# High and low V of one head as one stationary operand in attention's value products

## The chip, the cores and the metric

The kernel runs on one core of a Trainium2 chip. The core has five engines that run side by side, each through its own queue in order: TensorE (PE in the profile; PEld is its weight load), VectorE (DVE), ScalarE (ACT), GpSimd (POOL) and SyncE (SP), which here issues nearly all DMA transfers. They wait for one another through semaphores. The metric is the device time of one execution in microseconds; it is given as the median of several runs, and the profile is of one further execution.

## What is computed

Two layers on 512 tokens of width 1024, in float32. The change lies in the token mixer of the first layer, a stick-breaking attention with 16 heads of 64 columns; no softmax is taken. Cut to what matters:

```python
def stick_breaking_attention(q, k, v):
    ...
        z = jnp.einsum('bhtd,bhsd->bhts', q[:, :, q0:kend], k[:, :, :kend]).astype(jnp.float32) * scale
        ...
        before = s_idx < t_idx
        log_beta = jax.nn.log_sigmoid(z)
        log_1m = jnp.where(before, jax.nn.log_sigmoid(-z), 0.0)
        later = lax.cumsum(log_1m, axis=3, reverse=True) - log_1m
        a = jnp.where(before, jnp.exp(log_beta + later), 0.0)
        outs.append(jnp.einsum('bhts,bhsd->bhtd', a.astype(v.dtype), v[:, :, :kend]))
```

The last line, the product of the weights `a` with `v`, is what the change is about. Around it stand a QKV projection, an output projection, a SwiGLU feed-forward, a gated MLP mixer as the second layer's token mixer, a second feed-forward, and adaLN modulation before and after each.

## The kernel before

All large products run in TensorE's fp32r format on operands that are split in two: `split` (line 89) writes a rounded high part with ScalarE (line 93) and the remainder as a low part with VectorE (line 94). `mm3` (line 81) multiplies two such operands in three passes: high by high, high by low, low by high. Each pass is one matmul with its own weight load.

The kernel first normalizes and transposes the tokens, projects V's first half and q and k of head pair 0, then enters attention, in which heads are worked in eight pairs: one pair fills 128 columns of V (two heads of 64). V comes out of the projection in two halves of 512 columns; `v_evac` (line 568) splits each into tiles `Vh` and `Vl` of [128 tokens, two token blocks, 512 columns].

For a pair, `attend(i)` (line 721) gives four steps:

- `scores` (line 738): matmuls `z`, a sigmoid on ScalarE into `ga` (line 759), scans on VectorE into `left` (line 764), their differences on VectorE back into `ga` (line 769): the weights `a`.
- `flip` (line 775): transposes the weights of one head into the bank `tw`, and splits them into `ar` (high on ScalarE, low on VectorE).
- `values` (line 789): for each block of key tokens `jj`, `mm3` with 128 columns of V as the stationary operand and `ar` as the moving one, 128 or 256 columns of tokens wide, summed in the bank `av[h]`. The stationary columns are those of both heads; for each head `h` only the 64 rows of its own are used.
- `finish` (line 804): ScalarE copies for each head the 64 rows of its own from `av[h]` to `f` (line 810, `of` in the profile), and `split` writes the pair's output tile `o`.

Attention's queue on TensorE is written out by hand: with `pe["chain"]` set, every matmul is ordered behind the one before. The loop over pairs (from line 841) runs, for pair i: `flip(LATE)`, fillers, scores of pair i + 1 (first part), fillers, `values(LATE)`, `flip(EARLY[0])`, scores (second part), `values(EARLY[0])`, `flip(EARLY[1])`, scores (third part), `values(EARLY[1])`, `finish`. Each of the three `values` stages is called for both heads in turn; the text calls such a stage of two heads one call. `LATE` and `EARLY[0]` have, for a head, one block of 128 and one of 256 columns, `EARLY[1]` two of 256.

The fillers (line 674) are the projections of q and k of the later pairs (bank `pqk`) and, when these are done, a first part of the output projection (bank `y`). A filler step may also start a step of the adaLN modulation (`bg`, line 268): loads `rawada`, and a multiply-add into `G`, `A` and `B` on VectorE. Weights are loaded as `raw` and split into `wh` and `wl`, three tiles ahead.

On VectorE and ScalarE the order is set by a scheduler at build time, which takes the instruction that by its own estimates is ready first; so a new instruction also moves its neighbours.

Of the kernel before, what the change touches and what calls it, by code (L numbers as in the profile page):

```python
# [9 lines left out]
F32R = mybir.dt.float32r  # L10
AF = mybir.ActivationFunctionType
ALU = mybir.AluOpType

P = 128
T = 512
NT = T // P
# [9 lines left out]
def trunk(ctx: ExitStack, tc: tile.TileContext, A: dict, out: bass.AP):  # L26
# [16 lines left out]
    def nm(s):  # L43
        uid[0] += 1
        return f"{s}_{uid[0]}"

    def slot(dt, name, a=2, b=512):
        return s4.tile([P, a, b], dt, tag="s4", name=nm(name))

    def bank(name, tag="b"):  # L50
        return psum.tile([P, 512], F32, tag=tag, bufs=6 if tag == "b" else 2, name=nm(name))

    dve, act = nc.vector, nc.scalar
    pe = {"prev": None, "chain": False}

    def pe_op(b):

        if pe["chain"] and pe["prev"] is not None:
            order(b, pe["prev"])
        pe["prev"] = b  # L60

    def order(b, before):
        tc.add_manual_dep(
            b.ins, before.ins.name,
            mybir.DependencyInfo(mybir.DependencyClass.NoSync, mybir.DependencyReason.DATA),
            reason="order",
        )

    def mm(o, l, r, start, stop, after=None):
        b = nc.tensor.matmul(o, l, r, start=start, stop=stop, skip_group_check=True)  # L70
        pe_op(b)
        if after is not None:
            order(b, after)
# [3 lines left out]
    def transpose(o, i):  # L77
        last_tp[0] = nc.tensor.transpose(o, i, ident)  # L78
        pe_op(last_tp[0])

    def mm3(o, lh, ll, rh, rl, start, stop):
        mm(o, lh, rh, start, False)
        mm(o, lh, rl, False, False)
        mm(o, ll, rh, False, stop)
# [4 lines left out]
    def split(hi, lo, src, hi_dve=False):  # L89
        if hi_dve:  # L90
            dve.tensor_copy(hi, src)
        else:
            act.activation(hi, src, AF.Copy)  # L93
        dve.tensor_tensor(lo, src, hi.bitcast(F32), ALU.subtract)  # L94
# [453 lines left out]

    hT = new_hT()

    Vh = [[slot(F32R, "Vh") for _ in range(2)] for _ in range(2)]
    Vl = [[slot(F32R, "Vl") for _ in range(2)] for _ in range(2)]

    def v_step(vb, hf, k, w):
        for part in range(2):
# [11 lines left out]

    def v_evac(vb, hf):
        for tt in range(NT):
            split(Vh[hf][tt // 2][:, tt % 2, :], Vl[hf][tt // 2][:, tt % 2, :], vb[tt][:])  # L570

    onec = oneb[:, 0:1]

# [45 lines left out]
    vb = [bank("v0") for _ in range(NT)]  # L619
# [31 lines left out]
    st0.__exit__(None, None, None)  # L651
    fwork["raw"] = ctx.enter_context(tc.tile_pool(name="wraw2", bufs=2))
    v_evac(vb, 0)
    o8 = []
    with tc.tile_pool(name="att", bufs=1) as att, tc.tile_pool(name="att2", bufs=2) as att2:
# [65 lines left out]
        def attend(i):  # L721

            weights = {}
            vc = slice(i % 4 * P, (i % 4 + 1) * P)
            vhf = i // 4

            def layout(js):
                offs, N = {}, 0
                for j in js:
                    offs[j] = N
                    N += T - P * j
                return offs, N

            def scores(js):

                q, kt = qk[i]  # L740
                offs, N = layout(js)
                for j in js:
                    o, n = offs[j], T - P * j
                    js_ = slice(j * P, (j + 1) * P)
                    for t, (a, b) in enumerate(((0, 0), (0, 1), (1, 0))):
                        for h in range(2):
                            r = slice(64 * h, 64 * h + 64)
                            mm(
                                zb[h][:, o : o + n], q[r, a, js_], kt[r, b, j * P : T],
                                j == js[0] and t == 0, t == 2,  # L750
                            )
                wide = js[0] != 2
                g = att.tile(
                    [P, 2, T + 4 if wide else 260], F32, tag=f"ga{wide}",
                    bufs=3 if wide else 1, name=nm("ga"),
                )
                with tc.issue_after(table.ins):
                    for h in range(2):
                        last_act[0] = act.activation(g[:, h, :N], zb[h][:, :N], AF.Sigmoid, scale=-1.0)

                for h in range(2):
                    for e, j in enumerate(js):
                        o, n = offs[j], T - P * j
                        dve.tensor_tensor_scan(  # L764
                            left[:, h, o + 1 : o + e + 1 + n], g[:, h, o - e : o + n],
                            tri[:, 1 - e : n + 1], 1.0, ALU.mult, ALU.max,
                        )
                M = N + len(js) - 1
                dve.tensor_tensor(g[:, :, :M], left[:, :, :M], left[:, :, 1 : M + 1], ALU.subtract)
                for e, j in enumerate(js):  # L770
                    weights[j] = (g, offs[j] + e)

            turned = {}

            def flip(blocks, h):

                ps = tw[h]
                n = 0
                for jj, js in blocks:
                    for j in js:  # L780
                        g, o = weights[j]
                        o += (jj - j) * P
                        transpose(ps[:, n : n + P], g[:, h, o : o + P])
                        n += P
                ar = att2.tile([P, 2, T], F32R, tag="ar", name=nm("ar"))
                split(ar[:, 0, :n], ar[:, 1, :n], ps[:, :n])
                turned[blocks[0][0], h] = ar

            def values(blocks, h, stop):

                ar = turned[blocks[0][0], h]
                start = blocks is LATE
                n = 0
                for jj, js in blocks:
                    w = len(js) * P
                    mm3(
                        av[h][:, js[0] * P : js[0] * P + w],
                        Vh[vhf][jj // 2][:, jj % 2, vc], Vl[vhf][jj // 2][:, jj % 2, vc],
                        ar[:, 0, n : n + w], ar[:, 1, n : n + w],
                        start and n == 0, stop and jj == 3,  # L800
                    )
                    n += w

            def finish():
                o = slot(F32R, "o")
                o8.append(o)
                f = npool.tile([P, 512], F32, tag="n", name=nm("of"))
                for h in range(2):
                    r = slice(64 * h, 64 * h + 64)
                    act.activation(f[r, :], av[h][r, :], AF.Copy)  # L810
                split(o[:, 0, :], o[:, 1, :], f[:])

            return scores, flip, values, finish

        with tc.issue_after(last_sqrt[0].ins):
# [7 lines left out]
        vb = [bank("v1") for _ in range(NT)]  # L823
        zb = [bank("z") for _ in range(2)]
        bg.bank = lambda: zb[0]
        cur = attend(0)
        for k in range(KD):
            if k % 2 == 0:
                wv = wget(("wv", 1, k // 2))
            v_step(vb, 1, k, wv)  # L830
            if k in (1, 4):
                cur[0](B31 if k == 1 else B2)
            bg.step(1)
        v_evac(vb, 1)
        tw = [bank("tw") for _ in range(2)]
        av = [bank("av") for _ in range(2)]
# [4 lines left out]
        for i in range(NPAIR):  # L841
# [6 lines left out]
            if more:  # L848
                cur = attend(i + 1)
                cur[0](B31)  # L850
# [384 lines left out]
```

## Time and profile before

| | |
|---|---|
| median of 3 runs | 1181.23 us |
| lowest and highest | 1174.74 and 1182.79 us |
| the profiled execution, first to last instruction | 1176.5 us |
| V's projections and attention | about 60 to 269 us |
| matmuls in all | 7296 |
| matmuls of the value products | 288 |
| mean granted TensorE clock | 0.990 |

The page gives the profiled execution's span and no other time of it. A line of a timeline reads: start, duration, engine, line of the kernel, operation, output <- inputs, shape, count, and in brackets the idle time of the engine before it and what ended that. Matmuls are pipelined, so that their durations overlap: what one costs in a stream is the distance from its start to the next one's start. In a table of windows the numbers behind the stretch are its length, the busy time of PE, PEld, DVE, ACT and POOL with their instruction counts, the granted clock, the share of DMA and GB/s.

### The profile page before, as it was taken

The page shows a single profiled execution, that of the slowest core. Times are in us where ns is not written, and L with a number is a line of the kernel's source. Part 1 is how long each engine was busy: PE and PEld are TensorE (multiplying, and loading weights), DVE is VectorE, ACT ScalarE, POOL GpSimd, SP SyncE. Part 2 cuts the span into 40 slices and gives each one's busy share as a digit, 9 for nine tenths or more (in the row PEclk, how much of TensorE's full clock was granted, in tenths as well). Part 3 has the DMA queues.
Part 4 walks back from the last instruction along what each step waited for, and adds up shares of the span by engine and source line. Part 5 has one row for each costly group of instructions (what it writes and reads, how often), then busy time and mean ns, then how long its engine had stood idle before and what let it go on. Part 6 is the DMA issues. An engine that isn't in the chain of part 4 may idle for free.

```text
span 1176.5 us, 18192 instructions
## 1 busy us (share of the span) xinstructions
PE 1140.3 (97%) x7296; PEld 1011.7 (86%) x7296; DVE 884.8 (75%) x1171; ACT 557.8 (47%) x935; POOL 20.2 (2%) x35
## 2 busy tenths in 40 slices
PE   5999999999999999999999999999999999999997
PEld 4776778888999999998878887988999999988886
DVE  6888998875998988878686864668889898873213
ACT  6444444554665555563143633526555555572112
POOL 0100000000000000000000100001000000000000
PEclk8999999999999999999999999999999999999999
DMA  8666452113424444338886473324244544244211
GB/s 328 201 213 231 144 161 72 55 54 126 160 92 144 134 139 142 122 112 262 281 286 237 151 250 125 109 71 156 80 143 126 161 127 142 75 127 160 90 54 72
DMA packets 48777, 173.93 MB, mean 148 GB/s; under 512 B 5674, under 2 KB 6058, under 8 KB 48692
## 3 DMA queue, kind: packets, MB, share of 16 engines
q1 hardware_dynamic: 46964, 166.48, 43.7%
q0 software_dynamic: 1728, 6.29, 1.4%
q8 instruction: 57, 0.93, 0.3%
q14 instruction: 28, 0.23, 0.1%
HBM read 164.36 MB, written 8.39 MB: 147 GB/s over the span
## 4 chain that ended last, share of the span: by engine, by line
PE 73%; DVE 11%; DMA 10%; ACT 3%; issue 3%; SPq 0%; DVEq 0%; ACTq 0%
PE r L70 31%; PE y L70 20%; DMA rawada<-in_ada 5%; PE v L70 4%; PE pqk L70 4%; PE gu L70 4%; DVE wl L94 2%; PE av L70 2%; PE u L70 2%; DVE left L764 1%; PE z L70 1%; DVE B L268 1%; DMA raw<-in_wdown 1%; PE tw L78 1%; DMA raw<-in_win_v 1%
## 5 line engine op out<-in xcount | busy, mean ns | idle before, releaser
L70 PE MATMUL y<-wh,as 128*128 128x512 f32 x832 | 264.0, 395 | 0.4 <-ACT gu L964 0.4
L93 ACT ACTIVATE wh<-raw 128x1024 fp32r<-128x1024 f32 x112 | 118.3, 1060 | 215.4 <-PE y L70 102.7
L94 DVE TENSOR_TENSOR wl<-raw,wh 128x1024 fp32r<-128x1024 f32 x112 | 136.3, 1221 | 107.4 <-ACT wh L93 107.1
L70 PEld LDWEIGHTS y<-wh,as 128*128 128x128 f32 x832 | 156.2, 188 | 37.4 <-ACT gu L964 0.8
L70 PE MATMUL r<-Sh,wl 128*128 128x256 f32 x608 | 170.3, 280 | 0.0
L70 PE MATMUL r<-Sh,wh 128*128 128x256 f32 x608 | 170.0, 280 | 0.0
L70 PE MATMUL r<-Sl,wh 128*128 128x256 f32 x608 | 170.0, 280 | 0.0
L70 PE MATMUL y<-wl,as 128*128 128x512 f32 x416 | 164.4, 395 | 0.0
L94 DVE TENSOR_TENSOR wl<-f,wh 128x1024 fp32r<-128x1024 f32 x76 | 92.8, 1221 | 36.4 <-ACT wh L93 36.4
L70 PEld LDWEIGHTS r<-Sh,wh 128*128 128x128 f32 x608 | 114.7, 189 | 0.0
L93 ACT ACTIVATE wh<-f 128x1024 fp32r<-128x1024 f32 x76 | 80.7, 1061 | 71.4 <-PE r L70 64.9
L70 PEld LDWEIGHTS r<-Sl,wh 128*128 128x128 f32 x608 | 114.5, 188 | 0.0
L70 PEld LDWEIGHTS r<-Sh,wl 128*128 128x128 f32 x608 | 114.5, 188 | 0.0
L70 PEld LDWEIGHTS y<-wl,as 128*128 128x128 f32 x416 | 78.2, 188 | 18.0
L70 PE MATMUL r<-hTh,wh 128*128 128x256 f32 x304 | 89.0, 293 | 0.0
L70 PE MATMUL r<-hTl,wh 128*128 128x256 f32 x304 | 84.9, 280 | 0.0
L70 PE MATMUL r<-hTh,wl 128*128 128x256 f32 x304 | 80.2, 280 | 0.0
L70 PEld LDWEIGHTS r<-hTh,wh 128*128 128x128 f32 x304 | 57.2, 188 | 5.4 <-DVE gu L959 1.0
L70 PE MATMUL r<-hTh,b 128*128 128x256 f32 x304 | 60.7, 282 | 0.0
L70 PE MATMUL v<-wh,hTh 128*128 128x512 f32 x128 | 53.2, 416 | 6.0 <-ACT hTh L599 6.0
L70 PEld LDWEIGHTS r<-hTl,wh 128*128 128x128 f32 x304 | 57.4, 189 | 0.1
L93 ACT ACTIVATE wh<-rawx 128x1024 fp32r<-128x1024 f32 x38 | 40.4, 1063 | 35.2 <-PE r L70 30.9
(203 smaller groups left out, 2530.4 us busy)
## 6 DMA issues: line engine op xcount, KB each, us to landing
rawada<-in_ada SPq DMA_DIRECT2D x80, 512.0 KB, 4.5
raw<-in_wdown SPq DMA_DIRECT2D x44, 512.0 KB, 4.1
rawy<-in_wy SPq DMA_DIRECT2D x38, 512.0 KB, 3.7
rawx<-in_wx SPq DMA_DIRECT2D x38, 512.0 KB, 4.6
raw<-in_wqk SPq DMA_DIRECT2D x16, 512.0 KB, 4.8
ada<-in_ada0p SPq DMA_DIRECT2D x12, 512.0 KB, 8.2
raw<-in_wgu SPq DMA_DIRECT2D x12, 512.0 KB, 4.0
xd<-x POOLq DMA_DIRECT2D x12, 512.0 KB, 2.9
```

The costliest lines, as they stand in the source:

```text
L70: b = nc.tensor.matmul(o, l, r, start=start, stop=stop, skip_group_check=True)
L78: last_tp[0] = nc.tensor.transpose(o, i, ident)
L93: act.activation(hi, src, AF.Copy)
L94: dve.tensor_tensor(lo, src, hi.bitcast(F32), ALU.subtract)
L268: dve.scalar_tensor_tensor(acc, w, sc[:, kk : kk + 1], acc, ALU.mult, ALU.add)
L764: dve.tensor_tensor_scan(left[:, h, o + 1 : o + e + 1 + n], g[:, h, o - e : o + n], tri[:, 1 - e : n + 1], 1.0, ALU.mult, ALU.max,)
```

## The change

V's two tiles of a half become four, one for each block of 128 tokens (`V`, [128 tokens, four pairs, 256 columns]). For each pair the 256 columns are: high part of head 0, low part of head 0, low part of head 1, high part of head 1, 64 columns each. `v_evac` writes them with strided operands. So 128 neighbouring columns hold the high and low V of one head, and one pass with them as the stationary operand gives both products, in the two halves of the rows. `values` then takes two passes, with the high and the low part of `ar`, where it took three; the product of low by low, which was left out, comes with it. In `finish`, ScalarE copies the half of the rows with the low V's products to the rows of the other half, and VectorE adds the high V's products from PSUM.

```diff
-    Vh = [[slot(F32R, "Vh") for _ in range(2)] for _ in range(2)]
-    Vl = [[slot(F32R, "Vl") for _ in range(2)] for _ in range(2)]
+    V = [[slot(F32R, "V", 4, 256) for _ in range(NT)] for _ in range(2)]
...
     def v_evac(vb, hf):
         for tt in range(NT):
-            split(Vh[hf][tt // 2][:, tt % 2, :], Vl[hf][tt // 2][:, tt % 2, :], vb[tt][:])
+            v = V[hf][tt][:].rearrange("p a (b d) -> p a b d", b=4)
+            s = vb[tt][:].rearrange("p (a b d) -> p a b d", a=4, b=2)
+            split(v[:, :, 0::3, :], v[:, :, 1:3, :], s)
...
-            vc = slice(i % 4 * P, (i % 4 + 1) * P)
...
-                    mm3(
-                        av[h][:, js[0] * P : js[0] * P + w],
-                        Vh[vhf][jj // 2][:, jj % 2, vc], Vl[vhf][jj // 2][:, jj % 2, vc],
-                        ar[:, 0, n : n + w], ar[:, 1, n : n + w],
-                        start and n == 0, stop and jj == 3,
-                    )
+                    for part in range(2):
+                        mm(
+                            av[h][:, js[0] * P : js[0] * P + w],
+                            V[vhf][jj][:, i % 4, h * P : (h + 1) * P], ar[:, part, n : n + w],
+                            start and n + part == 0, stop and jj == 3 and part == 1,
+                        )
...
                 for h in range(2):
-                    r = slice(64 * h, 64 * h + 64)
-                    act.activation(f[r, :], av[h][r, :], AF.Copy)
+                    r, low = slice(64 * h, 64 * h + 64), slice(64 - 64 * h, 128 - 64 * h)
+                    act.activation(f[r, :], av[h][low, :], AF.Copy)
+                    dve.tensor_tensor(f[r, :], av[h][r, :], f[r, :], ALU.add)
                 split(o[:, 0, :], o[:, 1, :], f[:])
```

## The prediction

> **What bounds the kernel now.** The page comes first: TensorE is busy for nearly the whole span, VectorE for three quarters.
>
> ```profile
> span 1176.5 us, 18192 instructions
> PE 1140.3 (97%) x7296; PEld 1011.7 (86%) x7296; DVE 884.8 (75%) x1171; ACT 557.8 (47%) x935; POOL 20.2 (2%) x35
> ```
>
> So a matmul taken away is worth its time only where TensorE is not waiting. The view of the tile `av` shows what the edit touches and where it lies: between 112 and 269 us.
>
> ```profile
> L70 PE MATMUL av<-ar,Vh x192: 220/281/522, 112.2 to 268.3; 128*128 128x256 f32 x128, 128*128 128x128 f32 x64
> L70 PE MATMUL av<-ar,Vl x96: 272/281/416, 112.4 to 268.4; 128*128 128x256 f32 x64, 128*128 128x128 f32 x32
> L810 ACT ACTIVATE of<-av x16: 592/594/596, 130.7 to 268.7; 64x512 f32<-64x512 f32 x16
> ```
>
> That is 288 matmuls, 36 for each of eight head pairs. The windows, cut at one transpose batch of successive pairs (columns: length, then busy time of PE, weight load, VectorE, ScalarE), show two regimes.
>
> ```profile
> 145.75:167.90 22.15, 19.78 (x120) 15.60 (x118) 21.46 (x27) 10.20 (x19) 0.00 (x0) 1.00 0.59 176
> ...
> 189.68:211.25 21.57, 21.57 (x134) 17.54 (x133) 18.68 (x27) 11.62 (x21) 0.00 (x0) 1.00 0.23 74
> 211.25:232.79 21.54, 21.54 (x135) 17.54 (x133) 18.67 (x27) 12.10 (x22) 0.00 (x0) 1.00 0.16 49
> 232.79:250.71 17.92, 17.77 (x117) 14.34 (x116) 14.71 (x21) 9.41 (x18) 0.00 (x0) 1.00 0.26 89
> 250.71:268.70 17.99, 17.97 (x118) 15.32 (x116) 8.99 (x13) 8.59 (x15) 0.00 (x0) 1.00 0.00 0
> ```
>
> Up to 168 us VectorE is full (21.46 of 22.15) and TensorE has holes; after that TensorE is full and VectorE has some 3 us to spare per pair. TensorE's timeline names the holes and who ended them (in brackets: idle time, releaser):
>
> ```profile
> 105.34 0.50 PE L70 MATMUL pqk<-hTh,wh 128*128 128x512 f32 x1 [2.33 <-DVE q L662]
> ...
> 121.33 0.33 PE L70 MATMUL av<-ar,Vh 128*128 128x128 f32 x1 [1.91 <-DVE ar L94]
> ...
> 156.29 1.02 PE L70 MATMUL z<-k,q 64*128 64x128 f32 x10 [1.99 <-DVE k L94]
> ...
> 167.02 0.33 PE L70 MATMUL av<-ar,Vh 128*128 128x128 f32 x1 [0.38 <-DVE ar L94]
> ```
>
> All four are VectorE's. From 167 us on, none of this size is left.
>
> **The change, part by part.** *Value products.* Each pair runs three calls for two heads; each call takes 6 matmuls per head before and 4 after, so 12 become 8, on TensorE in the same place:
>
> ```order
> L70 MATMUL av_808<-ar_918,Vh_133 128x128 x2
> L70 MATMUL av_808<-ar_918,Vl_137 128x128
> L70 MATMUL av_808<-ar_918,Vh_133 128x256 x2
> L70 MATMUL av_808<-ar_918,Vl_137 128x256
> L70 MATMUL av_809<-ar_924,Vh_133 128x128 x2
> ```
>
> The same call of pair 0 after, both heads, on TensorE:
>
> ```order
> L70 MATMUL av_808<-ar_918,V_134 128x128 x2
> L70 MATMUL av_808<-ar_918,V_135 128x256 x2
> L70 MATMUL av_809<-ar_924,V_134 128x128 x2
> L70 MATMUL av_809<-ar_924,V_135 128x256 x2
> ```
>
> Only the passes with `Vl` are gone; nothing else on TensorE changes place. Their price is a start-to-start distance, since matmuls overlap: first a call of mixed shapes up to the transposes behind it, then a call of 256 columns alone.
>
> ```profile
> 188.14 0.33 PE L70 MATMUL av<-ar,Vh 128*128 128x128 f32 x2
> ...
> 189.52 1.03 PE L78 MATMUL tw<-identt,ga 128*128 128x128 f32 x8
> ...
> 194.99 0.40 PE L70 MATMUL av<-ar,Vh 128*128 128x256 f32 x2
> ...
> 196.41 0.81 PE L78 MATMUL tw<-identt,ga 128*128 128x128 f32 x6
> ```
>
> 12 in 1.38 us is 0.115 each, 12 in 1.42 is 0.118. Four fewer save 0.46, 0.46 and 0.47 us: 1.39 per pair, 11.1 over eight pairs. Both shapes cost alike, so I take the measured 0.115 for the narrow ones too. The Trainium skill ("TensorE: Matmul & The Clock Gate", section "Back-to-back issue gap") gives about 81 ns for a 128-column matmul in a stream with its weight load; by that the 32 narrow passes would be worth 0.034 us less each, and the whole saving an estimated 10.0 in place of 11.1. The rows here say 0.115.
>
> *End of a pair.* `finish` gains two VectorE additions on 64x512, and the scheduler moves its neighbours. VectorE, end of pair 2 (pairs 3 to 5 read alike), before:
>
> ```order
> L769 TENSOR_TENSOR ga_1484<-left 128x2x512
> L94 TENSOR_TENSOR k_1496<-pqk_1409,k_1496 128x512
> L94 TENSOR_TENSOR wl_1620<-raw_1617,wh_1619 128x1024
> L94 TENSOR_TENSOR ar_1533<-tw_806,ar_1533 128x384
> L94 TENSOR_TENSOR o_1524<-of_1525,o_1524 128x512
> L94 TENSOR_TENSOR ar_1539<-tw_807,ar_1539 128x384
> L764 SCALAR_TENSOR_TENSOR left<-ga_1560,tri 128x128
> ```
>
> VectorE at the same place after:
>
> ```order
> L769 TENSOR_TENSOR ga_1456<-left 128x2x512
> L94 TENSOR_TENSOR k_1468<-pqk_1385,k_1468 128x512
> L811 TENSOR_TENSOR of_1493<-av_808,of_1493 64x512
> L811 TENSOR_TENSOR of_1493<-av_809,of_1493 64x512
> L94 TENSOR_TENSOR ar_1503<-tw_806,ar_1503 128x384
> L94 TENSOR_TENSOR ar_1509<-tw_807,ar_1509 128x384
> L94 TENSOR_TENSOR o_1492<-of_1493,o_1492 128x512
> L94 TENSOR_TENSOR wl_1586<-raw_1583,wh_1585 128x1024
> L764 SCALAR_TENSOR_TENSOR left<-ga_1530,tri 128x128
> ```
>
> The additions stand ahead of `ar`, which the next value products need; the weight split `wl` goes behind `o`; the scan comes later by two additions. On ScalarE `o` goes behind both `ar`, so its wait for the additions holds up no `ar` there. Durations of one such cycle on VectorE:
>
> ```profile
> 193.52 2.34 DVE L764 TENSOR_TENSOR_SCAN left<-ga,tri 128x512 f32<-128x512 f32 x2 [1.45 <-ACT ga L759]
> ...
> 197.04 0.69 DVE L94 TENSOR_TENSOR k<-pqk,k 128x512 fp32r<-128x512 f32 x1
> 197.64 1.22 DVE L94 TENSOR_TENSOR wl<-raw,wh 128x1024 fp32r<-128x1024 f32 x1
> 198.77 0.55 DVE L94 TENSOR_TENSOR ar<-tw,ar 128x384 fp32r<-128x384 f32 x1
> ...
> 200.34 2.44 DVE L764 TENSOR_TENSOR_SCAN left<-ga,tri 128x128 f32<-128x128 f32 x4
> 202.70 0.67 DVE L327 TENSOR_TENSOR G<-z,g 128x512 f32<-128x512 f32 x1
> ...
> 206.10 1.23 DVE L94 TENSOR_TENSOR wl<-raw,wh 128x1024 fp32r<-128x1024 f32 x1 [0.99 <-ACT wh L93]
> ...
> 207.84 1.01 DVE L94 TENSOR_TENSOR ar<-tw,ar 128x384 fp32r<-128x384 f32 x2
> ...
> 212.35 1.29 DVE L94 TENSOR_TENSOR ar<-tw,ar 128x512 fp32r<-128x512 f32 x2 [0.39 <-ACT ar L93]
> 215.08 2.34 DVE L764 TENSOR_TENSOR_SCAN left<-ga,tri 128x512 f32<-128x512 f32 x2 [1.43 <-ACT ga L759]
> ```
>
> An addition of 512 columns with one operand in PSUM took 0.67 (`G`); queued one behind another such operations start 0.60 apart (197.04 to 197.64, `k` to `wl`). No row shows one on 64 partitions; ScalarE's `of` on 64 (0.594) is no cheaper than this, so I take 0.60, bounds 0.3 (half) and 0.7. Two: 1.2 per pair, 9.6 in all.
>
> *Does VectorE still fit after 167 us?* Scan to scan the cycle is 21.56, with 0.99 + 0.39 + 1.43 = 2.81 idle: 18.75 of work. With 1.2 it is 19.95, in a TensorE cycle of 21.56 - 1.39 = 20.17. It fits by 0.2. In detail: the additions push the later scan back 1.2, the 0.99 of idle time at `wl` takes up all but 0.2, so `ar` runs 208.05 to 209.06, its first half done at 208.6. TensorE comes to those products 0.93 earlier (two calls) than in this row:
>
> ```profile
> 209.72 0.33 PE L70 MATMUL av<-ar,Vh 128*128 128x128 f32 x2
> ```
>
> That is 208.79; the second head is asked for 0.5 later. It just passes. At 215.08 the remaining idle time brings VectorE back into step. So 17 calls (pair 2's last two, pairs 3 to 7) save 0.46 to 0.47: -7.9. One of them may be swallowed where the k path of pair 7 already holds TensorE: +0.5.
>
> *Up to 167 us* VectorE sets the pace, so saved passes are hidden and additions show: those of pairs 0 and 1, 4 x 0.6 = +2.4. Against it: in pair 2 one `wl` (1.14 start to start) now stands behind the `ar` waited for at 167: -1.1. And the call at 121.33 ran at a low clock:
>
> ```profile
> 119.30:121.30 2.00, 0.12 (x2) 0.00 (x0) 2.00 (x4) 0.00 (x0) 0.00 (x0) 1.00 0.68 182
> 121.30:125.00 3.70, 3.67 (x19) 3.67 (x20) 3.40 (x5) 0.40 (x1) 0.00 (x0) 0.56 0.63 224
> ...
> 153.00:157.00 4.00, 2.01 (x17) 1.40 (x15) 4.00 (x6) 1.03 (x3) 0.00 (x0) 1.00 0.60 194
> ```
>
> (the column before the last two is the granted clock). Its 12 matmuls took 2.18 (121.33 to 123.51, where the transposes start); four fewer are 0.7 off, and VectorE's next scan hangs on what follows. Sum +0.6. The swaps of q, `wl` and adaLN loads at 100 to 112 us only permute equal work: 0, bounds -1 and +1.
>
> *V's evacuation* keeps its count, with strides of 64 columns; taken as free, at most doubled for one half:
>
> ```profile
> 93.57 2.48 DVE L94 TENSOR_TENSOR Vl<-v,Vh 128x512 fp32r<-128x512 f32 x4
> ```
>
> so 0 to +2.5. *Last pair:* its output waits for two more additions, behind this much other TensorE work (98 matmuls, 0.233 each; the last pair's product comes 57 of them in, 13 us):
>
> ```profile
> 268.67 22.88 PE y L70 x98
> ```
>
> so free. Behind it the order on every engine is unchanged.
>
> Sum: -7.9 + 0.5 + 0.6 = -6.8. The profiled execution has only its span, 1176.5, which becomes 1169.7. The three runs before have a median of 1181.23, 4.7 above the span; the same difference gives 1174.4.
>
> **The rivals.** (1) *TensorE loses its clock.* Before 157 us the waits for VectorE grow, since it comes 0.5 later (pair 0's additions less the 0.7) and TensorE earlier: by three calls, 1.4, at pair 1's second call, a wait of up to 1.9; by two more, 0.9, at 156.29, a wait of 1.99 + 0.5 + 0.9 = 3.4 at most. A wait of 1.91 was followed by 3.7 us at 0.56 of the clock, one of 1.99 by none. Two more such stretches cost 3.7 x 0.44 = 1.6 each: 1177.6. The Trainium skill (same page, section "What's actually happening") lets the clock drop only after an idle window of about 3.4 us, free-running; by that rule waits of 1.9 cost no clock, and one of 3.4 stands at the edge; the stretch after the wait of 1.91 us does not agree with it.
>
> (2) *VectorE becomes the bound, slower.* Place: the scan-to-scan cycle of pairs 0 to 5. From an addition above 0.7 us, or idle time at `wl` that moves with TensorE, the 0.2 of room is gone; then 12 additions show (+7.2), only pairs 6 and 7 save (-2.8): +4.4, 1185.6. For it: the room is 1%. Against it: ScalarE's part comes earlier too. With several clock drops besides it could pass 1193.
>
> (3) *Everything counts:* VectorE's new order removes the early waits: -11.1, 1170.1. For it the earlier q at 105 us; against it VectorE's 97%.
>
> (4) *The passes are not cheaper*: the order shows 24 per pair, so this would need a longer pass; nothing speaks for it.
>
> **How the numbers follow.** Forecast 0.60; (1) 0.18; (2) 0.14, of it 0.03 over 1193; (3) 0.06; (4) 0.02. The runs before lie 8 us apart, so a median is open by 2 or 3. The forecast's own bounds (early part -2 to +4, V +2.5) give 1171 to 1180, and (1) and (3) lie inside once that is added: 1168.5 to 1182.5, leaving out most of (2). One per cent, about what a measurement of this kernel can tell from no change, is 11.8 us: to be faster by that needs more than all of the 11.1. So faster 0.05, within 0.91, slower 0.04.
>
> **What would show it.** 192 `av` matmuls at 0.115 to 0.118; additions of 0.60 apart; pair cycles of 20.2 after 170 us with TensorE full; a wait of up to 1.9 us at pair 1's second call. Wrong if waits for `ar` or `k` stay after 170 us, if the clock drops more than once, or if additions take over 0.7.

## The result and the profile after

| | before | after |
|---|---|---|
| median (8 runs each, taken side by side) | 1177.11 us | 1171.32 us |
| lowest and highest | 1174.74 and 1182.79 | 1168.44 and 1172.87 |
| ratio of the times | | 0.9943, 95% interval 0.9923 to 0.9963 |
| span of the profiled execution | 1176.5 us | 1170.6 us |
| time of that execution | not listed | 1172.87 us |

The changed kernel is 0.57% faster, some 6.7 us, with an interval of 4.4 to 9.1. That is within the 1% that the prediction counted as no change, but it is not nothing. The medians lie 5.8 apart. In the eight runs of the changed kernel the time is 2.2 to 2.3 us above the span, so the profiled execution of before took an estimated 1178.8.

First the page after: the span, and the busy time of each engine.

```profile
span 1170.6 us, 18007 instructions
PE 1131.0 (97%) x7200; PEld 1000.2 (85%) x7200; DVE 894.6 (76%) x1187; ACT 557.9 (48%) x935; POOL 20.2 (2%) x35
```

96 matmuls are gone (7296 to 7200) and 9.3 us of TensorE's busy time; VectorE has 16 instructions and 9.8 us more. The view of the tile `av` after:

```profile
L70 PE MATMUL av<-ar,V x192: 219/281/385, 114.8 to 262.6; 128*128 128x256 f32 x128, 128*128 128x128 f32 x64
L810 ACT ACTIVATE of<-av x16: 588/592/596, 128.8 to 262.9; 64x512 f32<-64x512 f32 x16
L811 DVE TENSOR_TENSOR of<-av,of x16: 671/688/695, 130.6 to 263.5; 64x512 f32<-64x512 f32 x16
```

The passes that are left are as long as before (281 ns median). What they cost in a stream is the distance to the transposes behind them, in TensorE's timeline after:

```profile
186.64 1.09 PE L70 MATMUL av<-ar,V 128*128 128x128 f32 x8
187.57 1.03 PE L78 MATMUL tw<-identt,ga 128*128 128x128 f32 x8
```

Eight passes in 0.93 us are 0.116 each, where twelve took 1.38 us. Now the windows, cut at the third transposes of each pair (columns as before). The same cuts in the kernel before give 23.44, 21.12, 21.57, 21.53, 17.93 and 14.45 us; the last two come first here.

```profile
232.62:250.55 17.93, 17.78 (x118) 14.35 (x116) 14.71 (x21) 9.41 (x18) 0.00 (x0) 1.00 0.26 89
250.55:265.00 14.45, 14.45 (x95) 12.25 (x94) 7.87 (x11) 6.91 (x12) 0.00 (x0) 1.00 0.00 0
```

The kernel after:

```profile
143.81:167.88 24.07, 21.24 (x118) 16.56 (x117) 23.33 (x30) 10.45 (x19) 0.00 (x0) 0.93 0.51 151
167.88:187.57 19.69, 19.69 (x120) 15.79 (x119) 19.16 (x27) 10.98 (x20) 0.00 (x0) 1.00 0.40 128
187.57:207.76 20.19, 20.19 (x122) 16.18 (x121) 19.25 (x29) 11.61 (x21) 0.00 (x0) 1.00 0.25 71
207.76:227.94 20.18, 20.18 (x122) 16.17 (x121) 19.81 (x30) 11.94 (x22) 0.00 (x0) 1.00 0.17 51
227.94:245.29 17.35, 16.69 (x105) 13.01 (x104) 16.36 (x24) 9.55 (x19) 0.00 (x0) 1.00 0.32 111
245.29:259.44 14.15, 13.32 (x83) 10.91 (x82) 10.06 (x15) 7.02 (x12) 0.00 (x0) 1.00 0.00 0
```

From 168 to 228 us TensorE is full and each pair is 1.43, 1.38 and 1.35 us shorter. That is the forecast's 1.39, and its cycle of 20.2. In the last two windows TensorE's holes have grown (0.66 and 0.83 us, where they were 0.15 and none), and only 0.58 and 0.30 us are won. TensorE's timeline after names the larger holes from 110 us on:

```profile
110.15 1.76 PE L70 MATMUL z<-k,q 64*128 64x128 f32 x10 [1.73 <-DVE k L94]
...
142.89 1.08 PE L70 MATMUL av<-ar,V 128*128 128x128 f32 x7 [1.87 <-DVE ar L94]
...
155.81 1.01 PE L70 MATMUL z<-k,q 64*128 64x128 f32 x10 [1.55 <-DVE k L94]
166.96 1.08 PE L70 MATMUL av<-ar,V 128*128 128x128 f32 x7 [1.29 <-DVE ar L94]
...
236.19 0.50 PE L70 MATMUL y<-wh,o 128*128 128x512 f32 x1 [0.57 <-DVE k L94]
...
254.15 1.08 PE L70 MATMUL av<-ar,V 128*128 128x128 f32 x7 [0.83 <-DVE ar L94]
```

The wait of 1.87 at pair 1's second call is the one that was forecast at "up to 1.9". The 0.57 at `y` was 0.15 before:

```profile
240.87 0.50 PE L70 MATMUL y<-wh,o 128*128 128x512 f32 x1 [0.15 <-DVE k L94]
```

The 0.83 at 254 us, in the first call of pair 7, was not foreseen.

**Attention in two parts.** To compare executions I measure from three rows: the third scores of pair 0, the third transposes of pair 2 (the cut), and the first row of the output projection's long run. After:

```profile
93.93 0.97 PE L70 MATMUL z<-k,q 64*128 64x512 f32 x6
...
167.88 1.03 PE L78 MATMUL tw<-identt,ga 128*128 128x128 f32 x8
...
262.86 22.62 PE y L70 x97
```

The early part (first to second row) is 73.95 us, the late part (second to third) 94.98. Before, the third row is the one at 268.67 that the prediction shows, and the first two are these:

```profile
92.75 0.97 PE L70 MATMUL z<-k,q 64*128 64x512 f32 x6
...
168.40 1.04 PE L78 MATMUL tw<-identt,ga 128*128 128x128 f32 x8
```

That makes 75.65 and 100.27. Both kernels were profiled a second time, and a third execution of the changed kernel's code up to the cut comes from an experiment below.

| execution | early part | late part | from the span's start to the first row | from the last row to the span's end |
|---|---|---|---|---|
| before | 75.65 | 100.27 | 92.75 | 907.8 |
| before, again | 75.13 | 100.28 | 90.50 | 905.6 |
| after | 73.95 | 94.98 | 93.93 | 907.7 |
| after, again | 77.18 | 95.03 | 92.48 | 904.6 |
| after up to the cut (third pass late) | 76.46 | | 90.97 | 906.5 |

The late part repeats to 0.05 us: it is 5.3 us shorter. The early part of the same code differs by 3.2 us from one execution to the next, and what lies outside attention by 2 to 3 us; a single profile can't show whether 1 us was won or lost there. The mean of the three early parts after is 75.9, against 75.4 before: +0.5, with a spread of 1.6 either way.

### The profile page after: what moved, and what is told of

Its sections match the earlier page's. It is cut to its first block, busy times and chain, and to the rows that moved or that the text cites. A ratio compares the mean times of both kernels' runs of the same rounds, so it can differ in the third digit from the quotient of the medians.

```text
span 1170.6 us, 18007 instructions
## 1 busy us (share of the span) xinstructions
PE 1131.0 (97%) x7200; PEld 1000.2 (85%) x7200; DVE 894.6 (76%) x1187; ACT 557.9 (48%) x935; POOL 20.2 (2%) x35
## 4 chain that ended last, share of the span: by engine, by line
PE 72%; DVE 12%; DMA 10%; ACT 3%; issue 3%; SPq 0%; DVEq 0%; ACTq 0%
PE r L70 32%; PE y L70 20%; DMA rawada<-in_ada 6%; PE v L70 4%; PE pqk L70 4%; PE gu L70 3%; DVE left L764 2%; DVE wl L94 2%; PE u L70 2%; DVE B L268 1%; PE av L70 1%; PE z L70 1%; DMA raw<-in_win_v 1%; PE tw L78 1%; ACT wh L93 1%
```

## The experiments

Each was timed beside the kernel before on the same chip; ratios are to that kernel.

**The two kernels again.** No edit: the changed kernel with several rounds, the kernel before for one more profile.

> The changed kernel once more, unaltered, for a second profile: how far the stretch up to 168 us (from pair 0's third scores to pair 2's last transposes, 73.95 us in its first profile) differs between executions. If the place of the low clock and of the adaLN loads decides it, it comes out 1 to 4 us longer, as in the kernel with the third pass in pairs 3 and 4, which is the same up to there (76.46); if the first profile is typical, within 0.5. From 168 us to the end of attention 94.98, within 0.1 in both cases.

> The kernel before once more, unaltered, for a second profile: the same stretch was 75.65 us; 1 us of difference or more if the clock and the loads decide it. From 168 us to the end of attention 100.27, within 0.1.

The changed kernel had a median of 1169.14 us, ratio 0.9927 (0.9901 to 0.9952); the profile of the kernel before had a span of 1171.5 us, 5.0 less than its first one, with attention 0.5 shorter. The table above holds both. The changed kernel's early part came out 3.2 longer, as the first case expected; the 1 us or more expected of the kernel before did not come (0.5). What follows: the late part carries the verdicts below, the early part only differences of 3 us and more.

**The additions alone.** To the kernel before, with its three passes:

```diff
-                    act.activation(f[r, :], av[h][r, :], AF.Copy)
+                    act.activation(f[r, :], av[h][r, :], AF.Copy, scale=0.0)
+                    dve.tensor_tensor(f[r, :], av[h][r, :], f[r, :], ALU.add)
```

> The kernel before with the two additions per pair alone: three passes and Vh/Vl stay, ScalarE's copy writes zeros (scale 0), and VectorE adds the PSUM rows to them, so that the output is the same. Theory A (VectorE sets the pace up to 168 us, TensorE after it): the additions of pairs 0 and 1, four of 0.71, show as about +2.5 to +3 by 168 us, and after that they are hidden but for up to 1 us in the last two pairs: attention ends 2.5 to 4 us later than before, the whole span at about 1179 to 1180.5. Rival B (TensorE sets the pace everywhere): 0 to +1. Rival C (VectorE sets the pace everywhere): 16 x 0.71 = +11.4, 1188.

1180.57 us, ratio 1.0042 (1.0021 to 1.0064). The early part is 79.00 us (+3.4 to +3.9 on the two executions of before), the late part 101.45 (+1.2). The early part's share is a little more than theory A gave (2.5 to 3), and it is about as large as the 3.2 by which executions of one code differed. The 16 additions have some 11 us of busy time, and the time shows 5.

**The passes alone.** In the changed kernel, ScalarE copies each head's own half of the rows and nothing is added, so that the products with the low V are left out of the result.

```diff
-                    act.activation(f[r, :], av[h][low, :], AF.Copy)
-                    dve.tensor_tensor(f[r, :], av[h][r, :], f[r, :], ALU.add)
+                    act.activation(f[r, :], av[h][r, :], AF.Copy)
```

> The changed kernel without the additions: each head's rows are copied from the high V's product alone, so the low part of V is left out of the output. Theory A: by 168 us about 2 us earlier than the changed kernel (2.9 of additions back, less a weight split that moves forward again), no wait for ar in pair 7 (0.8 back): span 1167 to 1168, some 9 us under before. Rival B: as the changed kernel, 1170 to 1171. Rival C: 11 us under the changed kernel, 1159.

1167.15 us, ratio 0.9918 (0.9889 to 0.9948). The late part is 93.90, 1.08 less than with the additions. Where that comes from stands in TensorE's timeline of this kernel, for pair 6's second call and pair 7's first:

```profile
241.79 1.08 PE L70 MATMUL av<-ar,V 128*128 128x128 f32 x8
242.71 1.03 PE L78 MATMUL tw<-identt,ga 128*128 128x128 f32 x8
...
250.52 1.36 PE L70 MATMUL av<-ar,V 128*128 128x128 f32 x8
```

Neither has a wait in it. The call at 241.79 takes 0.92; with the additions the same call takes 1.23, as the changed kernel's timeline shows (VectorE writes the `ar` of its second head at 244.2 to 244.8, while it runs):

```profile
244.06 1.39 PE L70 MATMUL av<-ar,V 128*128 128x128 f32 x8
245.29 1.04 PE L78 MATMUL tw<-identt,ga 128*128 128x128 f32 x8
```

The 0.31 there and the wait of 0.83 at 254 us are 1.14, which is the 1.08. Without additions, the wait of 0.57 at `y` stays: that one belongs to the saved passes.

With this version the late part comes apart into its two causes. The saved passes take 6.4 from it without the additions (100.27 to 93.90) and 6.5 with them (101.45 to 94.98); the additions put on 1.2 with three passes and 1.1 with two. The early part shows nothing so clear: 75.4 and 75.9 are the means of before and after, 79.00 has the additions alone, and this version has 75.20. Taking the additions out gave back 0.7 there, inside the spread, and not the 2 us of theory A.

**The third pass put back, early or late.** A third pass per block in two of the eight pairs, with the low part of `ar` once more as its moving operand, so that this term is counted twice there. Pairs 0 and 1:

```diff
-                    for part in range(2):
+                    last = 2 if i in (0, 1) else 1
+                    for part in range(last + 1):
...
-                            V[vhf][jj][:, i % 4, h * P : (h + 1) * P], ar[:, part, n : n + w],
-                            start and n + part == 0, stop and jj == 3 and part == 1,
+                            V[vhf][jj][:, i % 4, h * P : (h + 1) * P], ar[:, min(part, 1), n : n + w],
+                            start and n + part == 0, stop and jj == 3 and part == last,
```

> The changed kernel with a third pass put back in pairs 0 and 1 (24 matmuls more; it repeats the low part of the weights, which so counts twice there). Theory A: hidden behind VectorE, 0 to +0.7 against the changed kernel, span 1170.6 to 1171.3. Rival B: 24 x 0.116 = +2.8, 1173.4.

and the same edit with `i in (3, 4)`:

> The same third pass put back in pairs 3 and 4 (again 24 matmuls, the same repeated term). Theory A and rival B: +2.8 against the changed kernel, 1173.4, with pair cycles of 21.6 in place of 20.2 there. Rival C: hidden, 0 to +0.5.

Early: 1170.57 us, ratio 0.9943 (0.9921 to 0.9964), the same as the changed kernel's. Its early part of 77.10 lies within the spread of the changed kernel's three. One row shows where passes that were put back go, TensorE's wait at pair 1's second call:

```profile
142.67 1.54 PE L70 MATMUL av<-ar,V 128*128 128x128 f32 x11 [0.93 <-DVE ar L94]
```

In the three executions with two passes that wait is 1.87, 1.88 and 1.87. It is 0.93 here and still ends with VectorE's `ar`, so the passes ahead of it fill a wait. Late: 1173.22, ratio 0.9962 (0.9945 to 0.9980); the intervals of the two times overlap, but the windows do not leave it open. The full pair of the late version:

```profile
188.01:209.54 21.53, 21.53 (x135) 17.55 (x134) 19.78 (x29) 11.72 (x21) 0.00 (x0) 1.00 0.23 74
```

21.53 is the cycle of before again, against 20.19; with the calls in the windows on both sides (20.58 for 19.69, 20.62 for 20.18) the six calls cost 2.7 us, six times 0.45. So a pass pays in full after the cut. Before the cut no cost of the same 24 passes shows; with a spread of 1.6 in the early part and intervals of 2 to 3 us in the times, a part of their 2.8 could still be there.

**One addition of 128 rows.** ScalarE copies all four halves, VectorE adds once on all partitions:

```diff
+                    act.activation(f[r, 0, :], av[h][r, :], AF.Copy)
+                    act.activation(f[r, 1, :], av[h][low, :], AF.Copy)
+                dve.tensor_tensor(f[:, 0, :], f[:, 0, :], f[:, 1, :], ALU.add)
```

> ScalarE copies the rows of both products of both heads to SBUF (four copies of 64 rows in place of two), and VectorE adds all 128 rows in one operation. Theory: an addition of 64 rows took 0.71 because its rows start at another quadrant than those of the operation before; the one of 128 rows starts where its neighbours do, so it costs 0.60 start to start, and VectorE spends 0.83 less per pair: 1.7 us earlier than the changed kernel by 168 us and up to 0.8 in pair 7, span about 1168 to 1169. Rival: 0.71 is the price of any such addition, then 0.71 less per pair. Rival on the other side: ScalarE's two more copies (1.2 us) stand ahead of its ar and push that back by 1.2, as the additions did: no gain, 1170 to 1171.5.

1170.58 us, ratio 0.9941 (0.9925 to 0.9957): the same as the changed kernel. VectorE's timeline, first of the changed kernel, then of this one, shows what an addition costs:

```profile
195.09 0.68 DVE L94 TENSOR_TENSOR k<-pqk,k 128x512 fp32r<-128x512 f32 x1
195.69 1.40 DVE L811 TENSOR_TENSOR of<-av,of 64x512 f32<-64x512 f32 x2
197.12 1.02 DVE L94 TENSOR_TENSOR ar<-tw,ar 128x384 fp32r<-128x384 f32 x2
```

```profile
198.38 0.69 DVE L812 TENSOR_TENSOR of<-of 128x512 f32<-128x512 f32 x1
198.98 1.02 DVE L94 TENSOR_TENSOR ar<-tw,ar 128x384 fp32r<-128x384 f32 x2
```

Two additions on 64 rows take 1.43 us, 0.715 each; one on 128 rows takes 0.60. VectorE saves 0.8 per pair, and yet the late part (94.75) is only 0.2 shorter. Pair 6's second call is back at 0.92. At pair 7's first call most of the loss stays: from the transposes ahead of it to the next ones it is 5.97 us, where two additions make 6.12 and none 5.33. Now ScalarE's four copies, from 251.86 on, stand ahead of its `ar`, as the last rival had it:

```profile
254.29 0.87 ACT L93 ACTIVATE ar<-tw 128x384 fp32r<-128x384 f32 x2
```

Before the cut it gained nothing that shows either (77.02, where the theory had 1.7 us less).

**The addition on GpSimd.** The same four copies, and `nc.gpsimd.tensor_tensor` in place of the last line.

> The same four copies on ScalarE, and the addition of 128 rows on GpSimd, which is idle there. Theory A: VectorE is free of additions, so as the kernel without them: by 168 us 2 us earlier than the changed kernel, no wait in pair 7, span 1167 to 1168.5. Rival: ScalarE's two more copies push ar back and wait for nothing else, so 1169.5 to 1171; or GpSimd's addition slows VectorE's own operations beside it.

1172.69 us, ratio 0.9967 (0.9955 to 0.9980): the late part, 95.80, is 1.05 longer than with the one addition on VectorE, which was timed on the same chip. GpSimd's row, ScalarE's and VectorE's, at one pair's end:

```profile
199.35 1.83 POOL L812 TENSOR_TENSOR of<-of 128x512 f32<-128x512 f32 x1 [17.89 <-ACT of L811]
...
201.21 0.63 ACT L93 ACTIVATE o<-of 128x512 fp32r<-128x512 f32 x1 [1.04 <-POOL of L812]
...
201.88 0.69 DVE L94 TENSOR_TENSOR o<-of,o 128x512 fp32r<-128x512 f32 x1 [0.92 <-ACT o L93]
```

The addition takes 1.83 in place of 0.60. ScalarE's half of the split of `o` waits for it, and VectorE's half, which stands ahead of the next scan, waits for ScalarE's. Behind `o` on ScalarE stands the sigmoid `ga` (201.75); TensorE waits 0.40 us for that, at 202.38.

**The addition later in VectorE's queue.** The addition and the split of `o` are ordered behind the next pair's scans; those of pairs 0 and 1 are put off to pairs 4 and 5, where VectorE has room.

```diff
+                def fold():
+                    with tc.issue_after(last_ga[0].ins):
+                        dve.tensor_tensor(f[:, 0, :], f[:, 0, :], f[:, 1, :], ALU.add)
+                    o8[i] = slot(F32R, "o")
+                    split(o8[i][:, 0, :], o8[i][:, 1, :], f[:, 0, :])
...
+        LATER = {3: (2,), 4: (3, 0), 5: (4, 1), 6: (5,), 7: (6,)}
...
+            for j in LATER.get(i, ()):
+                folds[j]()
```

> Two passes, ScalarE's four copies into a tile that stays, and the one VectorE addition of 128 rows, with the split into o behind it, ordered behind the scans of the next pair; for pairs 0 and 1 they come only in pairs 4 and 5. If VectorE's queue up to 168 us is what hides the saved passes there (theory A), then taking 2 x (1.43 + 0.60) = 4.1 us of work out of it brings attention forward by 2 to 4 us before 168; pairs 4 and 5 get longer by up to 0.4 each (their VectorE work rises to 20.5 us); pair 7 has no wait for ar. Sum: 2.5 to 4 us under the changed kernel, 1167 to 1169. Rival: VectorE was waiting for the adaLN loads and for TensorE there, so that the work taken away leaves holes: within 1 us of the changed kernel.

1171.15 us, ratio 0.9951 (0.9929 to 0.9973): no gain. The early part is 75.07, below two of the three executions after and 0.8 below their mean, not the 2 to 4 us of the theory. The pairs that took the postponed additions have cycles of 21.30 and 21.25 in place of 20.2, and a new wait, in TensorE's timeline of this kernel:

```profile
204.78 0.50 PE L70 MATMUL z<-acch,ones 128*128 128x512 f32 x1 [0.52 <-ACT ga L761]
```

With a second addition and split VectorE is busy for 20.4 us in each of these two cycles, more than the 20.2 that a cycle lasted, and the late part grows from 95.0 to 97.84. So VectorE's room there is not enough.

**VectorE relieved of other work.** Eight multiply-adds into the modulation's `B` stand on VectorE at 137 to 165 us (1.28 us each). This edit was made once in the changed kernel and once in the kernel before: ScalarE takes the multiplication and GpSimd the addition.

```diff
-                    ada_stt(acc, raw, k)
+                    if (name, at) == ("B", 0):
+                        act.activation(raw, raw, AF.Copy, scale=sc[:, k : k + 1])
+                        nc.gpsimd.tensor_tensor(acc, acc, raw, ALU.add)
+                    else:
+                        ada_stt(acc, raw, k)
```

> The changed kernel, with the eight multiply-adds into B that stand on VectorE among the work of pairs 0 to 2 (1.2 us each, 9.6 in all) given to ScalarE (the multiplication, in place) and GpSimd (the addition). Computed is the same. Theory A (up to 168 us VectorE's queue sets the pace and hides the passes saved there): with 9.6 us less on VectorE the waits of TensorE for k and ar before 168 us shrink or go, so that this kernel is 2 to 5 us earlier there than the changed kernel, and it is ahead of the kernel before with the same edit by more than the changed kernel is ahead of the kernel before: 8 to 9.6 us in place of 5.8. Theory B (the early waits are those of a chain from one engine to the next, in which VectorE's amount of work does not count): the distance between the two stays at 5 to 7 us, and the waits stay. Theory C (GpSimd's additions of some 3.7 us each, one behind the other, or ScalarE's extra copies, end later than the work that needs B): both are slower than without this edit, by 2 us or more.

> The kernel before with the same edit alone: the eight multiply-adds into B of pairs 0 to 2 on ScalarE and GpSimd. Computed is the same. Theory A: 1 to 3 us faster than the kernel before, since TensorE, with three passes, has less early waiting to lose; the cut behind pair 1's last value products (third transposes of pair 2) comes 73 to 75 us behind the first scores in place of 75.1 to 75.7. Theory B: the same time as the kernel before within 1 us. Theory C: slower by 2 us or more, with waits for GpSimd or ScalarE in the rows.

With the change 1175.76 us, ratio 0.9993 (0.9978 to 1.0008); without it 1185.91, ratio 1.0090 (1.0067 to 1.0114). Both are slower than without the edit, by 5.9 and 9.8 us from the ratios, as the third theory had it. With it comes something that none of the three named: VectorE's own instructions get longer while GpSimd adds. GpSimd's and VectorE's timelines of the kernel before with this edit:

```profile
156.63 3.24 POOL L305 TENSOR_TENSOR B<-B,rawada 128x1024 f32<-128x1024 f32 x1 [1.10 <-ACT rawada L304]
161.60 6.10 POOL L305 TENSOR_TENSOR B<-B,rawada 128x1024 f32<-128x1024 f32 x2 [1.73 <-ACT rawada L304]
```

```profile
153.55 4.18 DVE L768 TENSOR_TENSOR_SCAN left<-ga,tri 128x512 f32<-128x512 f32 x2 [2.74 <-ACT ga L763]
157.76 3.19 DVE L773 TENSOR_TENSOR ga<-left 128x1024 f32<-128x1024 f32 x1
...
162.61 0.55 DVE L94 TENSOR_TENSOR ar<-tw,ar 128x384 fp32r<-128x384 f32 x1
163.07 2.40 DVE L94 TENSOR_TENSOR o<-of,o 128x512 fp32r<-128x512 f32 x1
```

The two scans took 2.34 elsewhere, the subtraction 1.22 and `o` 0.69. That lengthening takes up what VectorE was relieved of: in the early part of the kernel before it is busy for 72.2 us with the edit and for 71.3 and 71.7 without. The rest of the loss stands as VectorE's idle time, 12.7 us in place of 3.4 to 4.4; 11.1 of it are waits for ScalarE, whose multiplications wait for loads and for GpSimd. The late parts are 95.0 and 100.26, as without the edit; the early parts 80.8 and 85.0. So the distance between the two kernels grew to 10.2 us by the medians, but where the long GpSimd additions fall differs in the two, and the 4.1 of it that lie in the early part say nothing safe on the saved passes.

**VectorE relieved with nothing in its place.** The changed kernel without those eight multiply-adds.

```diff
-                    ada_stt(acc, raw, k)
+                    if (name, at) == ("B", 0):
+                        pass
+                    else:
+                        ada_stt(acc, raw, k)
```

> The changed kernel without the eight multiply-adds into B on VectorE at 137 to 165 us (1.28 us each, 1.19 start to start, 9.5 in all) and with nothing in their place; their loads stay. So the modulation's B is left out of the result. It puts the prediction's premise to the test by itself, without work on GpSimd: that VectorE's amount of work sets the pace up to the cut at pair 2's third transposes. Theory A (VectorE sets it): the stretch from the first scores to that cut, 73.95, 77.2 and 76.5 us in three executions of the same code, falls by 4 us or more, to 68 to 72; the time is 4 to 8 us under the changed kernel's, about 1163 to 1167, a ratio of 0.988 to 0.992; the stretch behind the cut stays at 95.0. Theory B (the order in which the engines hand work on, or the loads, set it): 74 to 77 us, the time that of the changed kernel, a ratio of 0.994.

1164.05 us, ratio 0.9878 (0.9857 to 0.9900). The three rows of this kernel:

```profile
91.93 0.97 PE L70 MATMUL z<-k,q 64*128 64x512 f32 x6
...
160.89 1.03 PE L78 MATMUL tw<-identt,ga 128*128 128x128 f32 x8
...
255.86 22.62 PE y L70 x97
```

The early part is 68.96 us, 5.0 to 8.2 below the three of the changed kernel; the late part is 94.97, unchanged. 9.5 us of work taken from VectorE shortened the early part by some 7 us. Of the four waits of TensorE between 110 us and the cut the first is left (1.75); one of 1.99 stands at pair 0's second call, where the changed kernel's second execution has 1.69. Of the 7 us, 2 to 3 are TensorE's own busy time (64.43 us, against 66.56 to 67.77 in the three), which stretches at a low clock lengthen (3.4 us here, 6.8 to 10.3 in the three); the rest is waiting. So a large cut in VectorE's work does move the pace there. The smaller ones did not show: 2 to 4 us less for VectorE gave 0.8 in the version with the later addition.

No version with the whole computation in it was faster than the changed kernel beyond the noise.

## Why the prediction was right, and which term was off

The time, 1171.32 us, lies 3.1 below the forecast of 1174.4 and within the range. The step from the profile to the median is what was off: it was taken as 4.7 and is 0.7, while the forecast for the profiled execution, 1169.7 of span, met 1170.6. The three runs that the forecast leaned on had a median 4.1 above that of all eight.

The mechanism, passes that pay where TensorE is full, is right. But all three signs that the prediction named for being wrong came: waits for `ar` and `k` after 170 us (0.83 and 0.57), two drops of the clock, and additions above 0.7. Each turned out small or, for the clock, not due to the change alone.

*Value products, 0.46 to 0.47 per call.* Right: 0.116 per pass, 1.43, 1.38 and 1.35 us per full pair, and 2.7 for six calls put back late. The estimate that went by 81 ns for the narrow passes (the Trainium skill, "TensorE: Matmul & The Clock Gate", section "Back-to-back issue gap") does not fit these rows: a call with half of its passes at 128 columns fell from 1.38 to 0.93 us.

*The additions at 0.60.* Too small: 0.715, above the upper bound of 0.7. The Trainium skill ("VectorE: DVE Perf Modes", section "Two Vector instructions with no wait between them") has a rule that gives this: an instruction whose operands start at another group of 32 partitions than those of the one before starts only when that one has finished. The first addition starts at partition 0, the second at 64, `ar` behind it at 0 again, and the addition of 128 rows, which starts at 0 like its neighbours, is back at 0.60. The trace agrees. The prediction took its price from neighbours that all start at partition 0.

*VectorE fits by 0.2 after 167 us.* Right for pairs 3 to 5, in spite of the dearer additions: VectorE still had idle time in front of the scan, down from 1.4 to 0.8 and 0.2.

```profile
191.57 2.34 DVE L764 TENSOR_TENSOR_SCAN left<-ga,tri 128x512 f32<-128x512 f32 x2 [0.81 <-ACT ga L759]
...
211.76 2.34 DVE L764 TENSOR_TENSOR_SCAN left<-ga,tri 128x512 f32<-128x512 f32 x2 [0.24 <-ACT ga L759]
```

So the second rival did not come true, though the price from which it was to decide (0.7) was passed: the idle time was larger than the 0.2 that the cycle's sum left.

*17 calls after 167 us, -7.9, and +0.5 at `y`.* This is the term that was mis-sized. Behind the cut lie 16 of the 17 calls: -7.4, with the +0.5 -6.9. The late part is 5.3 shorter, or 5.5 with one matmul of `y` that now runs ahead of its end (97 in place of 98, 0.23). The +0.5 came as forecast (0.15 to 0.57). Of the 1.4 that are missing, 1.1 lie in pair 6's second call and pair 7's first, where TensorE waits for VectorE's `ar`. The additions of pairs 5 and 6 stand on VectorE's path to `ar` as they do in the pairs before, but the cycles are shorter there (17.4 and 14.2 us in place of 20.2, with fewer projections between the calls), and TensorE comes before `ar` is ready. The prediction carried the fit over from pair 2's cycle to all later pairs and looked at the last pair only for its output. Leaving the additions out gave 1.08 back. The remaining 0.3 is open.

*Up to 167 us, +0.6.* The sign and size fit the mean (+0.5), but its parts can't be read off: the spread of 1.6 is larger. That VectorE's work sets the pace there is borne out by the execution without the `B` work (-7 us), and that saved passes go into its waits by the third pass put back in pairs 0 and 1 (a wait of 1.87 became 0.93). That the additions show there is not settled: +3.4 or more with three passes, 0.7 with two. So the +0.6 agreeing with +0.5 is luck, as far as these runs go.

*The first rival, a lost clock.* It takes part after all. The changed kernel's granted clock (the column before the last two) falls to half twice, after the waits of 1.73 and 1.87:

```profile
110.20:113.60 3.40, 3.40 (x14) 2.67 (x15) 3.40 (x5) 1.09 (x2) 0.00 (x0) 0.50 0.87 301
144.30:147.70 3.40, 3.40 (x12) 2.40 (x9) 3.40 (x5) 1.20 (x2) 0.00 (x0) 0.50 0.54 159
```

Its second execution has 3.4 us at half clock from 121.4 and 6.8 from 155.6, the latter around a wait of 3.15 at pair 2's k, which the prediction had bounded at 3.4. But the kernel before, which had one such stretch in its first profile, has two of 3.4 us in its second (from 102.7 and from 153.9), so two drops are no mark of the change. The rival's price of 3.2 us above the forecast shows in no mean: the early parts average what the forecast gave. That the two longer early parts of the changed kernel (77.18 and 76.46) have 10.2 and 10.3 us at half clock, and the shorter one (73.95) 6.8, can account for an estimated 1.7 of the difference (half of 3.4).

*V's evacuation, free.* Right for VectorE: it took 2.48 for four operations, as before. Whether the time behind attention is shorter by a microsecond with the new layout (904.1 to 907.7 in ten executions, 905.6 to 907.8 in four with the old one) is open.

Term by term, then: -5.5 late and +0.5 early is -5.0, near the lower end of the timed interval of 4.4 to 9.1. Whether the rest lies outside attention, which varies by more than that, is open. That the total gain of some 6.7 us meets the forecast's 6.8 so closely is in part luck, since the late term alone fell 1.4 short.

## What to carry to other kernels

Ask for each stage separately who is late: here the four passes saved in a call were worth their full 0.46 us where TensorE was full, and no gain could be measured where VectorE set the pace. What helped there was less work for VectorE, and much less (9.5 us); moving work to ScalarE, to GpSimd or to a later place in VectorE's own queue gained nothing in four attempts. When a new instruction stands ahead of one that others wait for, check the shortest cycle in which that happens, not the typical one. Price a vector operation by a row with the same start partition ahead of it and behind it, and profile a kernel more than once before reading a difference of 1 to 3 us out of a stretch that waits.

## What the runs showed of the hardware

- GpSimd's additions on SBUF operands hold up VectorE: a subtraction of two SBUF operands went from 1.22 to 3.19 us, `o` from 0.69 to 2.40, while `ar`, with one operand in PSUM, stayed at 0.55 beside the same additions (162.61, between 161.60 and 167.70 on GpSimd). The Trainium skill ("SBUF — State Buffer", section "SBUF: two separate sides") has the two engines lock a shared pair of ports for a whole instruction where VectorE reads two operands from SBUF; these rows agree.
- The length of a wait alone does not tell whether the clock falls. In the changed kernel waits of 1.73 us and of 1.87 (pair 1's second call) were followed by half the clock; in its second execution the same call waited 1.88 and kept the full clock, as it did after a wait of 2.11 at 108.9 us. The stretches at half clock have one length or a multiple of it: in the four profiles of the two kernels they last 3.4 us six times and 6.8 once, and in the kernel before with the additions on GpSimd one lasts 10.3 (157.9 to 168.2 us). They lie at other places in other executions of one code, and with them the early part differs.
- The same GpSimd addition of 128x512 took 1.27 to 2.29 us, two to four times VectorE's 0.60.
